# Two held sums that change places, a join moved by one slot, and a sum moved by one slot with a weight behind it

## The chip, the cores and the metric

The kernel runs on one core of a Trainium2 chip. The metric is the device time of one execution in microseconds; a stated time is the median of three runs unless it is said to be that of the profiled execution. Five engines of the core matter here: TensorE (PE in the profile; its weight loads are PEld), VectorE (DVE), ScalarE (ACT), GpSimd (POOL) and SyncE (SP), which issues nearly all DMAs.

## The reference

One layer of a hybrid block over a sequence of 1024 tokens with 1024 channels, in float32:

```
h = rms_norm(x, norm1_g);  z = h @ w_in              # 1024 x 7168 columns
glu_in, q, k, v, gate_logits = split(z)
a = a_val * sigmoid(a_gate)                          # GLU
a = silu(rms_norm(causal_depthwise_conv(a, width 31) + conv_b));  y_a = a @ w_conv_out
q, k = rms_norm per head (16 heads of 64)
for window, dilation in ((128, 1), (512, 4), (2048, 16)):   # three dilated windows, ALiBi slopes
    scores -> softmax -> o_g, lse_g
o = sum_g softmax(lse)_g * o_g;  y_b = o @ w_attn_out
x = x + (sigmoid(g_a) * y_a + sigmoid(g_b) * y_b) @ w_out
x = x + conv-GLU feed-forward (w_up, width-3 convolution, w_down)
```

## The kernel before

Every float32 product is made of three fp32r matmuls: an operand is split into a high part (a rounding copy, on ACT) and a low part (the rest, by a subtraction on DVE), and high x high, high x low and low x high are accumulated. `split` makes such a pair, `wpiece` loads a weight into one of four `raw` buffers, which are used in turn, and splits it.

The stages in order are: the first norm and the first GLU columns; the remaining GLU and half of the gate columns in pairs (71 to 285 us in the profile); Q, K and V, with the depthwise convolution on DVE, ACT and POOL beside both stages (to 567 us); the attention heads, with the other gate columns and the convolution's output product as filler (to 857 us); the merge of both branches; the output product; and the feed-forward part. In most of them the order of the instructions on ACT, DVE and PE (in the heads on POOL too) is the order written by hand (`tc.manual_schedule`); the other engines, SP's DMA queue among them, and the stretches between are ordered by a planner that simulates the kernel. `tc.issue_after(ins)` puts what is issued in its block behind `ins` on that engine.

**The pairs.** `PAIRS` has eleven pairs of column blocks, computed with a scheme of seven products instead of eight per pair: five GLU pairs, then six gate pairs. For each pair, PE accumulates into the PSUM bank X (half of `xz[n]`) and the bank Y (`spare_bank`), and two partial results are held in the two halves of the SBUF tile `pq`: `c12` (first half) and `p5` (second half). ACT copies X into `c12` (line 828), PE then forms Y, ACT copies Y into `p5` (line 834), PE goes on accumulating into X, DVE adds X to `p5` (line 719, a helper of `tt_`). For a gate pair `p5` is then spilled to DRAM (line 841); near the end of the pair DVE adds Y to `c12` and that is spilled (line 876). For a GLU pair, `last_v1` runs in the next pair: a sigmoid over `c12` in place (line 873), then one DVE product that reads both halves (line 874).

**The heads.** Work goes in slots, eight per head: slots 0 to 3 of a head score the first half of the queries, slots 4 to 7 the second half (slot 4 is the group "far", the second half's queries against the first half's keys at the larger dilation, lines 1091 to 1093). A slot on PE scores its blocks into one of two PSUM banks that alternate by slot (lines 1055, 1056); DVE takes the score plus mask and its minimum in one instruction (`least`, line 1059); ACT takes the exponentials (`powers`, line 1100). `BACK` = 12 slots later the same block is transposed on PE (`flip`, line 1152), split by ACT and DVE (lines 1173, 1174) and, one or two slots after that, multiplied with V (`weigh`, lines 1190, 1191). For the second half of the queries the far part and the rest have a softmax each, and the two are joined in between: DMAs bring each part's statistics to the other (lines 1117, 1120, 1124), `compare` (lines 1128, 1129, on DVE) runs at slot 4 + 8 of a head's own count, `combine` (one exponential on ACT, three DVE instructions to line 1137, then eight scalings on POOL, line 1103) one slot later. Slots in which a head is scored, and slots 12 later in which it is transposed, overlap with the next heads.

**The end of the heads.** Thirteen slots run after the last score. In some of them `o_step` advances the attention output's first half, in four parts: the sum of the two partial results that the heads left in DRAM (`raw_o`, line 1227, DVE), high part (line 1223, ACT) and low part (line 1220, DVE), each one step of `o_step` apart; a part's load is `o_fetch`. After that come the first four weights of the attention output (`ao_first`, `raw_ao`), planned behind the last low part (`settled_o[3]`), then the four parts of the second half through the same `raw` buffers, and the merge: sigmoids of two gates on ACT (lines 1342, 1343), PE's product `yb` into one of four banks (lines 131 to 133), and DVE's use of that bank (line 1351).

Of the kernel before, what the change touches and what calls it, by code (L numbers as in the profile page):

```python
# [15 lines left out]
AF = mybir.ActivationFunctionType  # L16
ALU = mybir.AluOpType
# [20 lines left out]
BACK = 12  # L38
# [31 lines left out]
def block_kernel(ctx: ExitStack, tc: tile.TileContext, x, xT, x0, g2, pack, mask,  # L70
                 w_first, w_ch, w_qkv, w_co, w_ao, w_o, w_up, w_down, out):
    nc = tc.nc
    act, dve, pool, pe, sp = nc.scalar, nc.vector, nc.gpsimd, nc.tensor, nc.sync
# [21 lines left out]
    shared = []  # L95
# [17 lines left out]
    def wpiece(src, name, raw=None):  # L113
        raw = stage(src, name) if raw is None else raw
        hi, lo = wsplit(raw, name)
        if len(src.shape) == 3:
            hi = hi.rearrange("p (a b) -> p a b", a=src.shape[1])
            lo = lo.rearrange("p (a b) -> p a b", a=src.shape[1])
        return hi, lo
# [199 lines left out]
    if True:  # L319
# [131 lines left out]
        turns = lambda t: t.rearrange("p (m s) -> p s m", s=2)  # L451
# [33 lines left out]
        a, b = range(4), range(4, 8)  # L485
# [91 lines left out]
        gating, ready = [True], []  # L577
# [191 lines left out]
        half_of = lambda c, half: apad[c][:, :, 15 + half * 256 : 15 + half * 256 + 256]  # L769
# [4 lines left out]
        with tc.issue_after(settled1.ins), tc.manual_schedule(engines=hand):  # L774
            padded(2)
            gv = [big_ps(f"glu{n}_2") for n in "gv"]
            for half in (1, 0):
                for ps, w in zip(gv, w2):
                    for _ in gemm_half(ps[:, half * 512 : half * 512 + 512], w, hT, half):
                        pass  # L780
            for n, which in ((0, 0), (0, 1)):
                load(n, which)
            token_sums(0)
            parts(0, 0, "v")
            token_sums(1)
            load(1, 0)
            sg = [cst.tile([P, 512], F32, tag="f2", bufs=2, name=f"sg_2_{half}") for half in range(2)]
            act.activation(sg[1], gv[0][:, 512:1024], AF.Sigmoid)
            sums(0)
            token_form("t2", 0)  # L790
            dve.tensor_tensor(out=half_of(2, 1), in0=turns(gv[1][:, 512:1024]), in1=turns(sg[1]), op=ALU.mult)
            token_form("t2", 1)
            act.activation(sg[0], gv[0][:, 0:512], AF.Sigmoid)
            dve.tensor_tensor(out=half_of(2, 0), in0=turns(gv[1][:, 0:512]), in1=turns(sg[0]), op=ALU.mult)
            parts(1, 0, "v")
            parts(0, 2, "s12")
            pair_first(0)
            for i in range(2):
                token_form("t1", i)
            pq = p1.tile([P, CW - 1 + T], F32, tag="apad", bufs=9, name="pq")  # L800
            c12, p5 = pq[:, 0:512], pq[:, 512:1024]
            parts(0, 1, "s3")
            begun(0)
            for i in range(2):
                token_form("t3", i)
            pair_first(1)
            for n, (a, b) in enumerate(PAIRS):
                X = xz[n][:, 0:512]
                Y = spare_bank
                (sh, sl), (gh, gl) = pw[n]["s12"], pw[n]["s3"]  # L810
                inner = 0 < n < N - 1
                glu = n < len(GLU)
                if n + 2 < N:
                    load(n + 2, 0)
                if n + 1 < N:
                    load(n + 1, 1)
                parts(n, "s4", "s4")
                if n == 0:
                    begun(1)
                    for i in range(2):  # L820
                        tt_(xts[1][2 + i], xts[0][2 + i], xts[1][2 + i], sub)
                if inner:
                    parts(n + 1, 0, "v")
                if 0 < n <= len(GLU):
                    last_v1()
                odd_add()
                product(X, sh[:, 4:8], sl[:, 4:8], *form["t2"], False)
                act.activation(c12, X, AF.Copy)
                if n == 0:
                    for i in range(2):  # L830
                        token_form("t4", i)
                conv(PULLS[0] if n else 0)
                product(Y, sh[:, 0:4], sl[:, 0:4], *form["t1"], True)
                act.activation(p5, Y, AF.Copy)
                conv(PULLS[1] if n else 0)
                if inner:
                    odd(ODD_PAIR[1], False)
                product(X, gh[:, 0:4], gl[:, 0:4], *b12, False)
                tt_(p5, X, p5, add)
                if not glu:  # L840
                    sp.dma_start(dgate[b - 16][:, 512:1024], p5)
                if n + 1 < N:
                    sums(n + 1)
                if inner:
                    pair_first(n + 1)
                    parts(n + 1, 2, "s12")
                    odd_add()
                    conv(PULLS[2])
                    begun(n + 1)
                    conv(PULLS[3])  # L850
                else:
                    product(Y, *pw[n]["s4"], *b22, False)
                    tt_(c12, Y, c12, add)
                    if n + 1 < N:
                        parts(n + 1, 2, "s12")
                paired = product(X, gh[:, 4:8], gl[:, 4:8], *form["t4"], False)
                if glu:
                    padded(b)
                    dve.tensor_tensor(out=half_of(b, 0), in0=turns(X), in1=turns(c11[n]), op=ALU.mult)
                else:  # L860
                    c21 = cst.tile([P, 512], F32, tag="f2", bufs=2, name=f"c21_{n}")
                    act.activation(c21, X, AF.Copy)
                    sp.dma_start(dgate[b - 16][:, 0:512], c21)
                if inner:
                    product(Y, *pw[n]["s4"], *b22, False)
                if n + 1 < N:
                    parts(n + 1, 1, "s3")
                odd(ODD_PAIR[0], False)
                if inner:
                    tt_(c12, Y, c12, add)  # L870
                if glu:
                    def last_v1(c=b):
                        act.activation(c12, c12, AF.Sigmoid)
                        shared[:] = [dve.tensor_tensor(out=half_of(c, 1), in0=turns(p5), in1=turns(c12), op=ALU.mult)]
                else:
                    sp.dma_start(dgate[a - 16][:, 512:1024], c12)
        for i in range(2):
# [21 lines left out]
        def qkv_tail(ch, tt, qn):  # L899
# [13 lines left out]
            for s, t in ((0, qh), (1, ql)):  # L913
# [13 lines left out]
        slots = [[wp.tile([P, 1024], F32R, tag=f"w{a}", bufs=4, name=f"qkv_{a}{i}") for a in ("hi", "lo")]  # L927
                 for i in range(4)]
# [98 lines left out]
    if True:  # L1027
# [81 lines left out]
        own, other, shares = {}, {}, {}  # L1109
# [99 lines left out]
        def o_fetch(half, k):  # L1209
            cs = slice(half * 512, half * 512 + 512)  # L1210
            part = lambda i: do_[k : k + 2, i, :, cs].rearrange("k p t -> p k t")
            raw = stage(part(0), f"o_{half}{k}").rearrange("p (a b) -> p a b", a=2)
            hi, lo = (oT[i][half][:, k : k + 2, :] for i in range(2))
            fetch(lo, part(1))
            return raw, hi, lo

        def o_step(new):
            if o_highs:
                raw, hi, lo = o_highs.pop()
                settled_o.append(dve.tensor_tensor(out=lo, in0=raw, in1=hi.bitcast(F32), op=ALU.subtract))  # L1220
            if o_sums:
                raw, hi, lo = o_sums.pop()
                act.activation(hi, raw, AF.Copy)
                o_highs.append((raw, hi, lo))
            if new:
                raw, hi, lo = new.pop(0)
                dve.tensor_tensor(out=raw, in0=raw, in1=lo.bitcast(F32), op=ALU.add)
                o_sums.append((raw, hi, lo))
# [10 lines left out]
        with tc.manual_schedule(engines={ENG.Activation, ENG.DVE, ENG.PE, ENG.Pool}):  # L1239
# [3 lines left out]
            for at in range(len(slots) + BACK + 1):  # L1243
# [34 lines left out]
                    result(*done)  # L1278
                    done = None
                for ago, ready in ((BACK - 3, combine), (BACK - 4, compare)):  # L1280
                    if 0 <= at - ago < len(slots) and slots[at - ago][1:] == (1, 0):
                        ready(slots[at - ago][0])
                for unit in new:
                    powers(*unit)
                if cur is not None and half == 0:
# [7 lines left out]
                    oT = [[hb2[0].tile([P, KT, 512], F32R, tag=f"hb{a}0", name=f"oT{a}0")] for a in range(2)]  # L1293
                    heads = [o_fetch(0, k) for k in range(0, KT - 2, 2)]
                if at - len(slots) in (4, 5, 8, 9, 10, 11, 12):
                    o_step(heads)
                if at == len(slots) + BACK - 4:
                    heads.append(o_fetch(0, KT - 2))
                if apart(at):
                    piece_low()  # L1300
                with tc.issue_after(last_v.ins) if not at else ExitStack():
# [19 lines left out]
    if True:  # L1321
        for a in range(2):
            oT[a].append(hb2_tile([P, KT, 512], F32R, f"hb{a}1", f"oT{a}1"))
        with tc.issue_after(settled_o[3].ins):
            ao_first = [wpiece(w_ao[c], f"ao{c}") for c in range(4)]
        for k in range(0, KT, 2):
            later = [o_fetch(1, k)]
            for _ in range(3):
# [606 lines left out]
```

## Time and profile before

| | |
|---|---|
| median of three runs | 1672.17 us (1672.17 to 1672.96) |
| profiled execution | 1673.21 us, span 1671.0 us |
| instructions | 23004 |
| granted TensorE clock | 1.000 |
| PE busy | 1658.8 us, 99% of the span |
| DVE busy | 1244.5 us, 74% |
| ACT busy | 918.8 us, 55% |
| POOL busy | 406.4 us, 24% |
| chain that ended last | PE 91%, DMA 3%, DVE 3%, ACT 1%, issue 1% |
| DMA over the span | 290.84 MB, 174 GB/s |

A busy share is an average over the stages. PE's share says that it is at work nearly all the time; where it is not, the list of who waited for whom names the places, and the timeline around each place shows what was in front. In a timeline row the columns are start, duration, engine, line, operation, result <- operands, shape and count; the bracket at the end is the engine's idle time before it and what ended it. A matmul's duration is modelled and longer than the step from one matmul to the next, so PE's idle times in brackets are shorter than the true gaps by the difference.

### The profile page before, as it was taken

Reading aid. Unit: us, or ns where it says so; the run is one execution under the profiler, and the core shown is the slowest. Engines: PE = TensorE matmul, PEld = TensorE weight load, DVE = VectorE, ACT = ScalarE, POOL = GpSimd, SP = SyncE. Lnnn points to the kernel's source line nnn. Section 1 sums busy time; section 2 is a strip of 40 time slices with the busy share of each in tenths; the row PEclk is TensorE's granted clock in tenths of the full one; section 3 lists DMA queues with packets and bytes.
Section 4 is the critical chain, followed back from the end, with each engine's and each line's share of the span. In section 5 each row is a group of like instructions: output and inputs, shape, how many; then the busy total and the mean of one; then the engine's idle time right before and its main releaser. Section 6 shows DMA issues by size and latency. Waiting matters only on the chain.

```text
span 1671.0 us, 23004 instructions
## 1 busy us (share of the span) xinstructions
PE 1658.8 (99%) x7867; PEld 1383.8 (83%) x7867; DVE 1244.5 (74%) x1996; ACT 918.8 (55%) x1748; POOL 406.4 (24%) x450
## 2 busy tenths in 40 slices
PE   9999999999999999999999999999999999999999
PEld 7888778888888888888888888888888888888887
DVE  6999887879784567867567645878776777789863
ACT  6555445776665578777646434555444544543431
POOL 0024344877752256455410000000000000000000
PEclk9999999999999999999999999999999999999999
DMA  9111335344345879888678594522222222598851
GB/s 358 39 51 51 100 108 198 95 131 163 114 133 182 303 237 299 264 262 246 173 266 288 202 327 167 176 86 89 89 76 88 76 86 90 162 390 293 281 171 51
DMA packets 182341, 290.84 MB, mean 174 GB/s; under 512 B 31952, under 2 KB 89936, under 8 KB 181712
## 3 DMA queue, kind: packets, MB, share of 16 engines
q1 hardware_dynamic: 180928, 285.05, 51.5%
q10 hardware_dynamic: 1296, 4.33, 0.6%
q8 instruction: 62, 1.02, 0.3%
q14 instruction: 55, 0.45, 0.1%
HBM read 209.50 MB, written 79.76 MB: 173 GB/s over the span
## 4 chain that ended last, share of the span: by engine, by line
PE 91%; DMA 3%; DVE 3%; ACT 1%; issue 1%; POOL 0%; SPq 0%; ACTq 0%; DVEq 0%; POOLq 0%
PE dx L1741 7%; PE xz L158 6%; PE xz L156 6%; PE xz L157 6%; PE dy L1741 5%; PE qkv L150 5%; PE qkv L148 5%; PE qkv L149 5%; PE y L158 2%; PE y L157 2%; PE y L156 2%; PE gx L156 2%; PE gx L158 2%; PE gx L157 2%; PE pp L1152 2%; PE wo L149 2%
## 5 line engine op out<-in xcount | busy, mean ns | idle before, releaser
L572 POOL TENSOR_TENSOR codd<-codd,cpart 128x513 f32<-128x513 f32 x112 | 147.8, 1321 | 136.3 <-DVE lo_s L100 58.6
L148 PE MATMUL qkv<-qkv_hi,hT 128*128 128x512 f32 x384 | 152.7, 398 | 0.0
L150 PE MATMUL qkv<-qkv_hi,hT 128*128 128x512 f32 x384 | 150.3, 391 | 0.0
L149 PE MATMUL qkv<-qkv_lo,hT 128*128 128x512 f32 x384 | 149.9, 390 | 0.0
L1644 DVE SCALAR_TENSOR_TENSOR u<-u,pk 128x1023 f32<-128x1023 f32 x88 | 112.1, 1276 | 1.2 <-ACT u L1642 0.9
L621 DVE SCALAR_TENSOR_TENSOR conv<-csum,both,conv 128x512 f32<-128x512 f32 x120 | 90.1, 751 | 2.3 <-ACT conv L653 0.3
L621 DVE SCALAR_TENSOR_TENSOR conv<-apad,pk,conv 128x512 f32<-128x512 f32 x120 | 90.0, 750 | 1.6
L150 PEld LDWEIGHTS qkv<-qkv_hi,hT 128*128 128x128 f32 x384 | 72.0, 188 | 15.7
L149 PEld LDWEIGHTS qkv<-qkv_lo,hT 128*128 128x128 f32 x384 | 72.3, 188 | 14.5
L148 PEld LDWEIGHTS qkv<-qkv_hi,hT 128*128 128x128 f32 x384 | 72.2, 188 | 14.2
L100 DVE TENSOR_TENSOR lo_uv<-raw_uv,hi_uv 128x1024 fp32r<-128x1024 f32 x20 | 24.5, 1225 | 79.6 <-ACT hi_uv L99 79.6
L1174 DVE TENSOR_TENSOR pl<-pp,ph 128x512 fp32r<-128x512 f32 (+1 forms) x95 | 58.8, 619 | 30.3 <-ACT ph L1173 29.3
L586 ACT ACTIVATE cpart<-apad,pk 128x513 f32<-128x513 f32 x112 | 76.6, 745 | 2.0 <-POOL codd L572 1.5
L1059 DVE CUSTOM_DVE_ANT_0 p<-s,m 128x512 f32<-128x512 f32 (+1 forms) x120 | 59.0, 502 | 21.8 <-POOL p L1103 16.6
L156 PE MATMUL xz<-h2left,hi_uv 128*128 128x512 f32 x176 | 68.6, 390 | 0.0
L156 PE MATMUL xz<-blk_t,hi_s3g 128*128 128x512 f32 x176 | 68.5, 389 | 0.0
L158 PE MATMUL xz<-blk_t,lo_s3g 128*128 128x512 f32 x176 | 68.5, 389 | 0.0
L157 PE MATMUL xz<-blk_t,hi_s3g 128*128 128x512 f32 x176 | 68.5, 389 | 0.0
L158 PE MATMUL xz<-h2left,lo_uv 128*128 128x512 f32 x176 | 68.5, 389 | 0.0
L157 PE MATMUL xz<-h2left,hi_uv 128*128 128x512 f32 x176 | 68.5, 389 | 0.0
L1173 ACT ACTIVATE ph<-pp 128x512 fp32r<-128x512 f32 (+1 forms) x95 | 51.1, 538 | 26.1 <-PE pp L1152 25.5
L124 POOL TENSOR_TENSOR rs<-ss,mhalf 128x8 f32<-128x8 f32 x32 | 53.6, 1676 | 36.5 <-DVE ss L123 34.4
(479 smaller groups left out, 5184.4 us busy)
## 6 DMA issues: line engine op xcount, KB each, us to landing
wr<-w_down SPq DMA_DIRECT2D x45, 512.0 KB, 5.6
kk<-dk SPq DMA_DIRECT2D x32, 512.0 KB, 6.1
gr<-dff SPq DMA_DIRECT2D x62, 256.0 KB, 5.4
raw_qkv<-w_qkv SPq DMA_DIRECT2D x24, 512.0 KB, 4.7
raw_g<-w_ch SPq DMA_DIRECT2D x23, 512.0 KB, 3.7
dff<-u SPq DMA_DIRECT2D x22, 512.0 KB, 2.6
raw_uv<-w_up SPq DMA_DIRECT2D x21, 512.0 KB, 3.6
raw_ug<-w_up SPq DMA_DIRECT2D x20, 512.0 KB, 3.6
```

Of the source, the lines that this page charges most:

```text
L148: pe.matmul(ps, ah, hi[:, k % 2, :], start=(k == 0), stop=False)
L149: pe.matmul(ps, ah, lo[:, k % 2, :], start=False, stop=False)
L150: end = pe.matmul(ps, al, hi[:, k % 2, :], start=False, stop=(k == KT - 1))
L156: pe.matmul(o, wh[:, k, :], bh[:, k, :], start=(start and k == 0), stop=False, skip_group_check=not start)
L157: pe.matmul(o, wh[:, k, :], bl[:, k, :], start=False, stop=False, skip_group_check=not start)
L158: end = pe.matmul(o, wl[:, k, :], bh[:, k, :], start=False, stop=(k == 3), skip_group_check=not start)
L572: r = pool.tensor_tensor(out=out, in0=in0, in1=in1, op=op)
L586: act.activation(part, zo[:, i : i + 513], AF.Copy, scale=taps[:, c, 2 * i + 1 : 2 * i + 2])
L621: dve.scalar_tensor_tensor(out=out_, in0=src[:, i : i + 512], scalar=w, in1=out_, op0=ALU.mult, op1=ALU.add)
L1059: dve.tensor_tensor_reduce(out=pt, in0=s, in1=m, scale=-1.0, scalar=3e38, op0=ALU.add, op1=ALU.min, accum_out=nm)
L1644: dve.scalar_tensor_tensor(out=acc[:, d:], in0=src[:, : T - d], scalar=w(2 - d), in1=acc[:, d:], op0=ALU.mult, op1=ALU.add)
L1741: pe.matmul(banks[n][:, cols], a[:, c], b[:, d], start=(start and i == 0 and m == 0), stop=(stop and i == nf - 1 and m == 2), skip_group_c ...
```

## The change

Three edits, in three places.

The first: the two halves of `pq` are put in a list `held`, and a pair with an odd number takes them in reverse order as `c12` and `p5`. `last_v1`, which runs in the next pair, is given the two halves of its own pair.

The second: in the slots before `BACK + 4` = 16, `compare` and `combine` look one slot further back, so for the first head they run one slot later, in slots 13 and 14 instead of 12 and 13. Later heads are as before.

The third: in the ninth slot after the last score `o_step` starts no new sum; the fourth sum, and its high and low part, come one slot later each. In the eleventh such slot the first attention-output weight `ao0` is loaded and split in the hand-written order, so its high part follows the fourth high part on ACT, and its low part stands ahead of the fourth low part on DVE. The other three weights stay behind that low part.

```diff
-            c12, p5 = pq[:, 0:512], pq[:, 512:1024]
+            held = [pq[:, 0:512], pq[:, 512:1024]]
...
                 (sh, sl), (gh, gl) = pw[n]["s12"], pw[n]["s3"]
+                c12, p5 = held[::-1] if n % 2 else held
...
-                    def last_v1(c=b):
-                        act.activation(c12, c12, AF.Sigmoid)
-                        shared[:] = [dve.tensor_tensor(out=half_of(c, 1), in0=turns(p5), in1=turns(c12), op=ALU.mult)]
+                    def last_v1(c=b, own=(c12, p5)):
+                        act.activation(own[0], own[0], AF.Sigmoid)
+                        shared[:] = [dve.tensor_tensor(out=half_of(c, 1), in0=turns(own[1]), in1=turns(own[0]), op=ALU.mult)]
...
                 for ago, ready in ((BACK - 3, combine), (BACK - 4, compare)):
-                    if 0 <= at - ago < len(slots) and slots[at - ago][1:] == (1, 0):
-                        ready(slots[at - ago][0])
+                    then = at - ago - (at < BACK + 4)
+                    if 0 <= then < len(slots) and slots[then][1:] == (1, 0):
+                        ready(slots[then][0])
...
                 if at - len(slots) in (4, 5, 8, 9, 10, 11, 12):
-                    o_step(heads)
+                    o_step(heads if at - len(slots) != 9 else [])
                 if at == len(slots) + BACK - 4:
                     heads.append(o_fetch(0, KT - 2))
+                if at == len(slots) + BACK - 1:
+                    ao_first = [wpiece(w_ao[0], "ao0")]
...
         with tc.issue_after(settled_o[3].ins):
-            ao_first = [wpiece(w_ao[c], f"ao{c}") for c in range(4)]
+            ao_first += [wpiece(w_ao[c], f"ao{c}") for c in range(1, 4)]
```

## The prediction

> **What bounds the kernel now.** I read the page first, then who waited for whom on PE, then the chain of waits in order of time, then the timeline at each place where PE stands still.
>
> ```profile
> PE 1658.8 (99%) x7867; PEld 1383.8 (83%) x7867; DVE 1244.5 (74%) x1996; ACT 918.8 (55%) x1748; POOL 406.4 (24%) x450
> ...
> PE gx L156 <- ACT pq L828: 3.3, 4, 1.6
> PE s L1055 <- DVE own L1059: 2.1, 1, 2.1
> PE o L1191 <- DVE pl L1174: 1.3, 1, 1.3
> ...
> PE yb L131 <- DVE gg L1351: 0.2, 1, 0.2
> ```
>
> PE is the bound at 99%, and the diff removes no matmul. So all it can win is PE's pauses, and these four rows, 6.9 us of 1671, are most of them. The first three are the three edited places. What counts at each is not whether the named wait goes, but which wait ends last once it is gone.
>
> **Part A: the two held sums change places from pair to pair.**
>
> ```profile
> 192.74 5.25 DMA dgate<-pq
> ...
> 196.57 0.39 PE L157 MATMUL spare<-gt,hi_s 128*128 128x512 f32 x1
> 196.79 0.39 PE L158 MATMUL spare<-gt,lo_s 128*128 128x512 f32 x1
> 198.10 0.60 ACT L828 ACTIVATE pq<-gx 128x512 f32<-128x512 f32 x1 [4.80 <-DMA dgate<-pq]
> 198.59 0.59 ACT L834 ACTIVATE pq<-spare 128x512 f32<-128x512 f32 x1
> 198.75 0.50 PE L156 MATMUL gx<-hT,hi_s 128*128 128x512 f32 x1 [1.57 <-ACT pq L828]
> 199.09 0.39 PE L157 MATMUL gx<-hT,hi_s 128*128 128x512 f32 x1
> 201.89 0.69 DVE L719 TENSOR_TENSOR pq<-gx,pq 128x512 f32<-128x512 f32 x1 [3.50 <-PE gx L158]
> L841 SPq DMA_DIRECT2D dgate<-pq x6: 319/320/376, 181.7 to 281.6; - x6
> DMA to landing us min/median/max: 2.0/2.6/9.9
> ```
>
> In a pair of gate columns the copy of X into `c12` (L828) cannot start until the spill of the previous pair's `c12` has been read out: ACT stands 4.80 us, PE needs X back and stands too. PE's steady step is 0.23 us (196.57 to 196.79; the starts are rounded), so the pause at 198.75 is 198.75 - 196.79 - 0.23 = 1.73 us. The list counts from a matmul's modelled end, 0.39 after its start, so its 3.3 us over four pauses is 3.3 + 4 x 0.16 = 3.95 us, and each restart costs 0.11 more (198.75 to 199.09 is 0.34). Together 4.4 us.
>
> After the edit, `c12` of a pair goes where the pair before held `p5`, whose spill (L841) left at 181.7 for the pair shown, 11 us before `c12`'s own spill and so more than 11 us before the new copy; the longest landing of any spill of this tile is 9.9 us. So this wait goes. What is late next: the copy into `p5` (L834) now meets the late spill. It could start when product Y ends, 196.79 + 0.39 = 197.2, and waits to 198.1. Behind it on ACT stand convolution copies, which started after 198.59 + 0.59 before and so lose nothing. Its reader is the sum at L719, which waited 3.50 us for PE and can now start at 201.89 - 1.84 = 200.05; `p5` is there by 198.1 + 0.6 = 198.7. Covered by 1.3 us. For the five GLU pairs the last product of the pair before reads both halves in one DVE instruction, so the exchange changes nothing there: 0. If the two halves were tracked as one tile, A would be worth 0; against a loss stands that no instruction is added. I take 4.4, ends 0 and 4.4.
>
> Arriving 4.4 us early could uncover the depthwise convolution, which POOL and DVE run beside. Its consumer is at 512.5:
>
> ```profile
> 506.64 1.29 POOL L572 TENSOR_TENSOR sqacc<-sqacc,csq 128x512 f32<-128x512 f32 x1
> 512.51 1.84 PE L685 MATMUL conv<-ones,sqacc 128*128 128x1 f32 x16
> ```
>
> POOL's sum ends at 507.9, 4.6 us ahead of PE, and DVE and ACT, which feed it, follow PE's order. A's gain stays.
>
> **Part B: the first head's softmax join, one slot later.**
>
> ```profile
> 580.00:600.00 20.00, 17.84 (x101) 14.70 (x100) 12.90 (x53) 13.99 (x43) 9.67 (x16) 1.00 0.65 189
> ...
> 587.27 0.39 PE L1055 MATMUL s<-kk,q 128*128 128x512 f32 x1
> 591.86 0.17 DVE L1128 TENSOR_TENSOR both<-own,other 128x8 f32<-128x8 f32 x1 [3.88 <-DMA dstat<-own]
> 592.14 0.68 DVE L1059 CUSTOM_DVE_ANT_0 p<-s,m 128x512 f32<-128x512 f32 x1
> 592.75 0.55 DVE L1174 TENSOR_TENSOR pl<-pp,ph 128x384 fp32r<-128x384 f32 x1
> 592.89 0.39 PE L1055 MATMUL s<-kk,q 128*128 128x256 f32 x1 [2.14 <-DVE own L1059]
> 593.73 0.51 DVE L1059 CUSTOM_DVE_ANT_0 p<-s,m 128x384 f32<-128x384 f32 x1
> 593.91 1.41 POOL L1103 TENSOR_SCALAR pf_first<-pf_first,both 128x128 f32<-128x128 f32 x4 [6.05 <-DVE both L1137]
> 595.29 2.16 POOL L1103 TENSOR_SCALAR p_first<-p_first,both 128x512 f32<-128x512 f32 x4
> 595.68 0.60 PE L1152 MATMUL pp_far<-ident,pf_first 128*128 128x128 f32 x4
> 597.62 0.60 PE L1152 MATMUL pp<-ident,p_first 128*128 128x128 f32 x4
> ```
>
> `compare` (L1128) holds DVE 3.88 us until the other half's statistics land; behind it stands the minimum L1059 over a score that PE wrote at 587.27, and PE waits for that bank: 2.14 + 0.16 = 2.3 us, 2.4 with the restart. One slot later, that minimum (0.68) and a low half (0.55) run before `compare`, in its waiting time, and this wait goes. But the landing does not move, and the join feeds what PE transposes next. Chain after: `compare` at 591.86 as now, then the next slot's minimum (0.51) and low half (0.55) instead of 0.68 + 0.55, then `combine`: it ends 0.17 earlier. POOL's scalings then end near 597.3 instead of 595.29 + 2.16 = 597.45, and the transposes at 597.62 need the last of them for their second block, 0.1 later. With PE 2.3 us early it stops at 595.68 - 2.3 = 593.4 for `pf_first` (last piece at 593.91 + 1.41 - 0.17 = 595.15) and again for `p_first`: the pause moves, and that second block's 597.7 becomes about 597.4. I take 0.3; ends 0 (nothing but the landing counts) and 2.4 (POOL's part would not count). SP: its spills of the next head's statistics and the loads behind them wait for exponentials that come up to 4 us earlier now; that may help later heads a little, and I leave it out of the sum.
>
> **Part C: the last sum of the heads' parts a slot later, a weight behind it.**
>
> ```profile
> 852.00:856.00 4.00, 2.86 (x15) 2.40 (x16) 3.99 (x6) 3.35 (x5) 0.00 (x0) 1.00 0.65 201
> 866.00:868.00 2.00, 2.00 (x11) 1.65 (x10) 0.98 (x1) 0.00 (x0) 0.00 (x0) 1.00 1.05 407
> ...
> 851.39 1.22 DVE L1227 TENSOR_TENSOR raw_o<-raw_o,oT 128x1024 f32<-128x1024 f32 x1 [1.05 <-DMA oT<-do]
> 851.41 0.42 PE L1190 MATMUL o<-ph,v 128*128 128x384 f32 x1
> 853.14 0.44 PE L1191 MATMUL o<-pl,v 128*128 128x384 f32 x1 [1.31 <-DVE pl L1174]
> 854.23 0.69 DVE L1174 TENSOR_TENSOR pl<-pp,ph 128x512 fp32r<-128x512 f32 x1
> 854.98 0.38 PE L1191 MATMUL o<-pl,v 128*128 128x256 f32 x1
> 855.97 2.35 DVE L100 TENSOR_TENSOR lo_ao<-raw_ao,hi_ao 128x1024 fp32r<-128x1024 f32 x2
> ...
> 856.11 5.52 DMA raw_ao<-w_ao
> 864.42 8.90 DMA oT<-do
> ...
> 876.51 2.28 SPq L104 DMA_DIRECT2D raw_ao<-w_ao  x4
> 879.16 0.50 PE L131 MATMUL yb<-oT,hi_ao 128*128 128x512 f32 x1 [0.19 <-DVE gg L1351]
> ```
>
> The sum L1227 waits for a landing and holds DVE; the low half `pl` behind it is late; PE loses 853.14 - 851.41 - 0.23 = 1.5 us. In the new order DVE, free at 851.39 - 1.05 = 850.34, does `pl` (0.55, above), a low part (1.2, half of the 2.35), the sum (1.22, its data landed) and the next `pl` (0.69): 3.66 us, less 0.07 where one starts before the other's end (592.14 + 0.68 against 592.75), done near 853.8. PE wants that one at 851.6 + (854.98 - 853.14) = 853.4, so 0.4 comes back at once; 1.1 is left.
>
> But the chain of waits runs from here through DMA to PE's pause at 879.16 (0.19 + 0.16 + 0.11 restart = 0.46): a weight's load leaves at 856.11 when the last low part has freed its buffer, and its split frees the buffer of the last second-half part, loaded at 864.42. The new order puts the weight's high and low part ahead of that last low part. After the sum (now ended near 853.1) come a high part, the weight's high part, its low part and then the last low part, at most 1.2 us each: it ends near 857.7, and that load leaves 1.6 us later. Two ends: the whole 1.6 arrives at 879.16 (C = -1.6), or nothing does and both pauses go (C = 1.1 + 0.46 + the 0.4 = 1.9). I take a value by the nearest row: at 866 the DMA share is 1.05 at 407 GB/s and the part needs 8.90 us, so it stands in a full queue, about 3.6 MB deep, and leaving 1.6 us later does not change when the queue gets to it. On the other side the third weight leaves about 2 us earlier, into the stretch at 852 to 856 where the share is only 0.65. So PE resumes near 879.0 whenever it arrives: C = 0.2.
>
> [...]
>
> **Sum.** 4.4 + 0.3 + 0.2 = 4.9 us. The profiled execution took 1673.21 us (span 1671.0), 1.04 above the median of 1672.17; taken from the median it gives 1667.3.
>
> **Rivals.**
> 1. The pauses go whole: POOL's scalings or the queue do not hold PE. 4.4 + 2.4 + 0.2 to 1.9 is 7.0 to 8.7: 1663.5 to 1665.2. For it: the list names DVE, not POOL. Against: 597.45 against 597.71.
> 2. The later weight arrives in full, or the queue runs dry before the parts: C = -1.6 to -3 (the dry time, 0.35 x 4 us, added). Sum 1.7 to 3.1: 1669.1 to 1670.5.
> 3. A does nothing because the halves count as one tile: 0.5 us, 1671.7. Against: the copy of `p5` ran at 198.59 right behind the other.
> 4. Slower. Only ACT, DVE, PE and POOL are ordered by hand, and only up to there; what follows is placed by a planner that sees a changed end. If it puts the splits of the second four weights (issued from 876.51; at 5.52 us for the first and 1.29 for each 512 KB behind it at 407 GB/s the last lands near 885.9) ahead of the first gates' sigmoids on ACT, PE resumes near 889, with 3 of the 5.84 us behind it that now lie between the last part's landing (864.42 + 8.90) and 879.16. That is 10 us lost: 1672.17 - 4.7 + 10 = 1677. It decides for slower from 8 us on. Against: before, they are issued last.
>
> The Trainium skill, TensorE: Matmul & The Clock Gate, Part 1, halves PE's clock after some 3.4 us without work; by that a pause as in rival 4 costs about 1.7 us more. No pause here is that long: the stretch with the longest shows 1.00.
>
> **How the numbers follow.** Forecast 0.52 (own range 1666.0 to 1668.8), rival 1 0.16, rival 2 0.17, rival 3 0.05, rival 4 0.06, small reorderings 0.04. 0.2% is 3.3 us, about what a measurement of this kernel can tell from no change. Faster: forecast, rival 1 and part of the rest, 0.73; same: rivals 2 and 3, 0.20; slower 0.07. The range 1663.8 to 1670.0 takes the forecast, nearly all of rival 1 and most of 2.
>
> **What would show it.** A: no row of PE waiting for L828, and L834 waiting for the DMA. B: PE waiting at L1152 for POOL, near 1.7 us; DVE's minimum ahead of L1128. C: no 1.3 us row at L1191, a longer one at `yb`. Wrong if PE waits longer at `yb` than it saved, or if L1152 shows no wait.

## The result, and the profile after

The changed kernel took 1668.26 us in the median of ten runs (1665.41 to 1669.63), the kernel before 1672.17 us (1670.07 to 1673.68); the ratio, taken over all the runs and so not quite that of the two medians, is 0.9975, with a 95% interval of 0.9966 to 0.9985, a gain of 4.2 us (2.5 to 5.7). The prediction was 1667.3 us, a gain of 4.9. The profiled execution of the changed kernel took 1668.18 us (span 1666.0). Lines behind the edits are one to four higher than before: L828 is L829, L1059 is L1060, L1152 is L1153, L1191 is L1192, L1351 is L1355.

PE's busy time is the same within 1 us, 1658.0 us. The list of PE's waits has changed in all three edited places:

```profile
PE yb L131 <- DVE gg L1355: 1.2, 1, 1.2
PE glu L446 <- ACT whi_gv L436: 1.1, 1, 1.1
...
PE pp_far L1153 <- POOL pf_first L1104: 0.7, 1, 0.7
PE o L1192 <- DVE pl L1175: 0.2, 1, 0.2
```

`gx` no longer waits for the copy out of X, the score no longer waits for DVE, and `o` waits 0.2 us instead of 1.3. In their place stand a wait for POOL at `pp_far` and a longer one at `yb`.

Edit 1, in the timeline of the changed kernel at the pair that the prediction showed:

```profile
195.52 0.60 ACT L829 ACTIVATE pq<-gx 128x512 f32<-128x512 f32 x1 [1.20 <-PE gx L158]
...
197.81 0.39 PE L158 MATMUL spare<-gt,lo_s 128*128 128x512 f32 x1
198.04 0.39 PE L156 MATMUL gx<-hT,hi_s 128*128 128x512 f32 x1
198.66 0.60 ACT L835 ACTIVATE pq<-spare 128x512 f32<-128x512 f32 x1 [2.54 <-DVE conv L621]
```

The copy follows the product (it waits for PE, not for the spill) and ends at 196.12, 1.9 us before PE needs X: 197.81 to 198.04 is PE's ordinary step. The second copy (L835) starts 0.46 us after the product's end (198.20); the list names DVE, but the late spill also landed only then, at 198.56. PE does not wait for it.

Edit 2, in the timeline of the changed kernel around the first head's join:

```profile
584.60 0.69 DVE L1060 CUSTOM_DVE_ANT_0 p<-s,m 128x512 f32<-128x512 f32 x1
588.71 0.17 DVE L1129 TENSOR_TENSOR both<-own,other 128x8 f32<-128x8 f32 x1 [2.69 <-DMA dstat<-own]
590.62 1.41 POOL L1104 TENSOR_SCALAR pf_first<-pf_first,both 128x128 f32<-128x128 f32 x4 [6.11 <-DVE both L1138]
591.05 1.37 PE L1153 MATMUL pp_far<-ident,pf_first 128*128 128x128 f32 x4 [0.72 <-POOL pf_first L1104]
592.01 2.16 POOL L1104 TENSOR_SCALAR p_first<-p_first,both 128x512 f32<-128x512 f32 x4
593.77 1.00 PE L1153 MATMUL pp<-ident,p_first 128*128 128x128 f32 x4
```

The minimum runs in the waiting time (584.60), DVE still waits for the landing, and PE follows POOL piece by piece: `pp_far` takes 1.37 us instead of 0.60, the second `pp` 1.00 instead of 0.60. A comparison of the two traces matmul by matmul (start after minus start before) shows it as a sum: -3.4 us ahead of the join, -5.8 with the score's pause gone, -3.9 behind `pp_far`, -3.5 behind `pp`. Of the 2.4 us, 2.3 come back within 5 us.

Edit 3, in the chain of waits of the changed kernel from the last head to PE's pause at `yb`:

```profile
850.35 1.24 DVE lo_ao L100
851.60 4.69 DMA raw_ao<-w_ao
...
857.40 1.24 DVE lo_ao L100
859.07 9.14 DMA oT<-do
868.30 1.24 DVE raw_o L1228
869.57 0.59 ACT oT L1224
870.65 1.28 ACT L1346
871.94 0.72 ACT gg L1346
872.67 0.62 ACT gg L1347
873.31 0.70 DVE gg L1355
874.06 0.50 PE yb L131
```

A weight's low part (857.40) is the last thing ahead of the load, as foreseen. That weight's own load left at 851.60, when the first weight's low part (850.35) had freed a buffer, and not behind the last low part of the sums, as the prediction had it. Between the landing at 868.21 and PE lie 5.85 us of DVE, ACT (L1346 at 870.65 is a table load for the sigmoid) and DVE again. By matmuls the difference of the traces goes from -4.8 before the heads' end to -6.0 behind it and to -5.1 behind `yb`: the heads' end gains 1.2 and `yb` takes 0.9 back.

### The profile page after: what moved, and what is told of

Its sections match the earlier page's. It is cut to its first block, busy times and chain, and to the rows that moved or that the text cites. A ratio compares the mean times of both kernels' runs of the same rounds, so it can differ in the third digit from the quotient of the medians.

```text
span 1666.0 us, 23008 instructions
## 1 busy us (share of the span) xinstructions
PE 1658.0 (100%) x7867; PEld 1384.3 (83%) x7867; DVE 1244.6 (75%) x1996; ACT 919.6 (55%) x1748; POOL 406.5 (24%) x450
## 4 chain that ended last, share of the span: by engine, by line
PE 96%; DMA 1%; DVE 1%; issue 1%; ACT 1%; POOL 0%; SPq 0%; POOLq 0%; DVEq 0%; ACTq 0%
PE dx L1745 7%; PE xz L156 6%; PE xz L158 6%; PE xz L157 6%; PE dy L1745 5%; PE qkv L150 5%; PE qkv L148 5%; PE qkv L149 5%; PE gx L158 3%; PE gx L156 3%; PE gx L157 3%; PE y L156 2%; PE y L158 2%; PE y L157 2%; PE pp L1153 2%; PE wo L150 2%
## 5 line engine op out<-in xcount | busy, mean ns | idle before, releaser
L1060 DVE CUSTOM_DVE_ANT_0 p<-s,m 128x512 f32<-128x512 f32 (+1 forms) x120 | 59.1, 503 | 21.7 <-POOL p L1104 16.2
```

Source lines behind the costliest of these rows:

```text
L1060: dve.tensor_tensor_reduce(out=pt, in0=s, in1=m, scale=-1.0, scalar=3e38, op0=ALU.add, op1=ALU.min, accum_out=nm)
```

## The experiments

**The three edits one by one, and the kernel before once more.** All are compared with the same runs of the kernel before (1672.83 us).

Edit 1 alone:

```diff
-            c12, p5 = pq[:, 0:512], pq[:, 512:1024]
+            held = [pq[:, 0:512], pq[:, 512:1024]]
...
+                c12, p5 = held[::-1] if n % 2 else held
...
```

> The kernel before with the first edit alone: the two held sums change places from pair to pair. Theory 1 (each edit acts at its own place, and the later pauses of the heads were shortened by the second edit): the four pauses behind the copy of X are gone, 4.5 us in the trace between the first and the last pair; the 2.3 us pause at 593 stays, the pauses near 661 to 675 stay at about 1.3 us in all, those at 851 and 879 stay. Median near 1672.2 - 4.5 = 1667.7. Theory 2 (the 1.3 us near 661 to 675 belong to the first edit, or come and go from execution to execution): they are gone or changed here too.

Measured: 1668.4 us (1666.83 to 1672.72), ratio 0.998 (0.9971 to 0.9988), a gain of 3.3 us (2.0 to 4.8). PE waits for L829 nowhere; at the score it still waits 2.7 us, at `o` 1.2. At one of the gate pairs the second copy waits for the late spill, as the prediction had foretold, and PE does not wait for that copy:

```profile
198.45 0.60 ACT L835 ACTIVATE pq<-spare 128x512 f32<-128x512 f32 x1 [2.91 <-DMA dgate<-pq]
```

Edit 2 alone:

```diff
-                    if 0 <= at - ago < len(slots) and slots[at - ago][1:] == (1, 0):
-                        ready(slots[at - ago][0])
+                    then = at - ago - (at < BACK + 4)
+                    if 0 <= then < len(slots) and slots[then][1:] == (1, 0):
+                        ready(slots[then][0])
```

> The kernel before with the second edit alone: the first head's join one slot later. Theory 1: the pause for the score's bank goes and comes back at the far part's transposes and at the next ones, net 0.0 to 0.3 us there; then 1.3 us more near 661 to 675, because SP's queue, which stood behind exponentials held up by the join, sends the next heads' loads earlier. Median near 1670.8. Theory 2: nothing near 661 to 675, median near 1672.1.

Measured: 1670.57 us (1668.52 to 1672.47), 0.9989 (0.9981 to 0.9998), a gain of 1.8 us (0.3 to 3.2). At its own place the trace gives 0.3 us: against the kernel before, its matmuls start 0.3 us earlier ahead of the join, 2.6 behind the score and 0.6 behind `pp`. The runs give more than the place.

Edit 3 alone:

```diff
-                    o_step(heads)
+                    o_step(heads if at - len(slots) != 9 else [])
...
+                if at == len(slots) + BACK - 1:
+                    ao_first = [wpiece(w_ao[0], "ao0")]
...
-            ao_first = [wpiece(w_ao[c], f"ao{c}") for c in range(4)]
+            ao_first += [wpiece(w_ao[c], f"ao{c}") for c in range(1, 4)]
```

> The kernel before with the third edit alone: last sum a slot later, the first weight behind it. Theory 1: the pause of 1.5 us at the heads' end becomes 0.25, and the pause before the fifth product of the merge becomes 1.3 instead of 0.35, because what it waits for comes out of a full DMA queue at the same time as before; net 0.2 to 0.4 us, median near 1671.9. Theory 2 (the pause at the merge in the changed kernel was lengthened by another edit): net 1.2 us or more, median 1671.0 or below.

Measured: 1671.44 us (1669.93 to 1674.86), 0.9997 (0.9988 to 1.0006). Its trace has both sides in PE's waits:

```profile
PE yb L131 <- DVE gg L1353: 2.1, 1, 2.1
...
PE o L1191 <- DVE pl L1174: 0.2, 1, 0.2
```

What `o` gains (1.3 to 0.2) `yb` takes, and more (0.2 to 2.1). By the starts of the matmuls this execution loses 0.6 us between the heads' end and `yb`, where 0.2 to 0.4 had been expected as a gain.

The kernel before, unchanged:

> The kernel before, unchanged, for a second trace of it beside the single edits: how much its pauses and its first loads differ from one execution to the next. Theory 1: the pauses at 198 to 278, 593, 661 to 675, 851 and 879 are the same within 0.2 us, and only the time of the first matmuls (PE's waits for the first weights, 0 to 2 us) differs. Theory 2: the pauses near 661 to 675 differ by a microsecond.

Measured: 1672.41 us (1671.35 to 1673.13), 1.0001 (0.9992 to 1.0009). It shows two things that one profiled execution of the kernel before had not. First, some of what separates the two first traces belongs to no edit. Some 1.3 us of short pauses between 661 and 675 us, absent after the change, are mostly absent here too and with each edit alone; so a theory that an edit brings that gain falls. And the pause of the pairs, 3.3 us in the list before, is smaller in each of the other traces that have it:

```profile
PE gx L156 <- ACT pq L828: 2.7, 4, 1.4
PE s L1055 <- DVE own L1059: 2.3, 1, 2.3
```

It is 2.5 us with edit 2 alone and 2.1 with edit 3 alone. Second, in the timeline of this execution PE is slow after the pause at the score:

```profile
592.62 0.39 PE L1055 MATMUL s<-kk,q 128*128 128x256 f32 x1 [2.28 <-DVE own L1059]
...
593.43 0.42 PE L132 MATMUL gate<-hT,hi_gt 128*128 128x512 f32 x1
593.66 0.61 PE L133 MATMUL gate<-hT,lo_gt 128*128 128x512 f32 x1
...
595.99 0.63 PE L1055 MATMUL s<-kk,q 128*128 128x512 f32 x1
...
596.84 0.73 PE L1152 MATMUL pp_far<-ident,pf_first 128*128 128x128 f32 x4
```

Matmuls of 512 columns follow at 0.43 us instead of 0.23, from 593.7 to 596.8. The windows of the same trace give the granted clock (the third number from the end):

```profile
592.00:594.00 2.00, 1.39 (x7) 1.27 (x8) 1.93 (x9) 1.40 (x4) 0.36 (x2) 0.92 0.00 0
594.00:597.00 3.00, 3.00 (x9) 2.36 (x8) 1.13 (x5) 2.17 (x7) 3.00 (x8) 0.50 0.48 133
597.00:600.00 3.00, 3.00 (x21) 2.72 (x20) 2.03 (x6) 2.17 (x5) 2.54 (x4) 0.99 0.87 283
```

Half clock from 594 to 597. Over the whole span this is a mean granted clock of 0.999 (1.67 us in 1671), and every timed run lists that mean. Of the 74 runs of the kernel before in all three sets of runs, 42 are at 1.000 (median 1671.36 us) and 32 below (1673.56). So the hypothesis was: the pause at the score costs not only its 2.4 us but, in about half of the executions, 2 us more, and edit 2, which only breaks the pause into pieces, takes these away. The next experiments ask for it from both sides.

**The statistics read earlier, without edit 2 and with it.** SP issues the read of the far half's statistics (`other<-dstat`) one slot earlier for the first head, ahead of the next head's loads:

```diff
-                for ago, n0, send in ((2, 0, far_out), (1, 3, near_to_far), (READ, 0, far_to_near)):
+                for ago, n0, send in ((2, 0, far_out), (1, 3, near_to_far), (READ - (at < BACK), 0, far_to_near)):
```

> The changed kernel, with SP's read of the far half's statistics (other<-dstat) issued one slot earlier for the first head, ahead of the next head's loads instead of behind them. The theory (the end of part B's wait is the landing, as the prediction's lower end says): the landing, which ends DVE's wait at L1129 at 588.71, comes about 3 us earlier, so the join's scalings on POOL end earlier by more than the pauses at pp_far (0.7 + 0.35 us) and at pp: both go, about 2 us less than the changed kernel, 1666.3 by the fast runs of it. The rival (POOL's scalings or DVE's order hold PE whenever the landing comes): the row of pp_far <- pf_first stays at 0.4 us or more and the time is that of the changed kernel, 1668.3.

Measured: 1666.73 us (1665.68 to 1669.74), 0.9967 (0.9956 to 0.9978). The timeline of the compare in this kernel:

```profile
587.44 0.17 DVE L1129 TENSOR_TENSOR both<-own,other 128x8 f32<-128x8 f32 x1 [2.06 <-DMA other<-own]
```

The landing came earlier by 1.3 us, not 3, and it is another DMA that ends it now: the near half's statistics (`other<-own`), which I had not counted, stand behind the same loads. PE waits 0.9 us at the score instead of 0.7 at `pp_far`, and gains 0.6 us on the changed kernel across the join. The time lies 1.5 us under the changed kernel's, with overlapping intervals; the place accounts for 0.6 of it.

The same without edit 2:

> Edits 1 and 3 with the early read, and without edit 2: the join stays in its old slot and the statistics come earlier. Two things are asked. If DVE stood at the compare for the landing alone, the pause of 2.1 to 2.7 us at the score's matmul (s <- own) is gone or below 0.5 us, 2.4 us of edit 2's upper end without edit 2. And the clock: without edit 2 the kernels ran about half of their executions below a granted clock of 1.000 (before 16 of 35, edit 1 alone 5 of 12, edit 3 alone 6 of 11), with it 1 of 21. Theory: it is the unbroken pause of 2.3 us or more that drops the clock; without that pause nearly all executions show 1.000, and the time is 1666 to 1667. Rival: the clock comes from somewhere else (edit 2's different order, or the chip's temperature); then about half stay below 1.000 and the median is 1 us higher.

Measured: 1668.73 us (1666.73 to 1671.99), 0.9977 (0.9967 to 0.9987). The pause did not go, for the same reason:

```profile
588.10 0.17 DVE L1129 TENSOR_TENSOR both<-own,other 128x8 f32<-128x8 f32 x1 [4.13 <-DMA other<-own]
...
589.13 0.39 PE L1056 MATMUL s<-kk,q 128*128 128x256 f32 x1 [2.36 <-DVE own L1060]
```

So it could not test the clock by removing the pause. It tests it in the other direction: pause 2.36 us, no edit 2, and 7 of 10 runs below 1.000 (their median 1669.85 us, that of the other three 1667.89).

**The join's combine right behind its compare**, on top of the change:

```diff
-                for ago, ready in ((BACK - 3, combine), (BACK - 4, compare)):
-                    then = at - ago - (at < BACK + 4)
+                joins = ((BACK - 3, combine), (BACK - 4, compare))
+                for ago, ready in joins[::-1] if at < BACK + 4 else joins:
+                    then = at - ago - (at < BACK + 4 and ready is compare)
```

> The changed kernel, with the first head's combine right behind its compare in the same slot, instead of a minimum and a low half between them: POOL's scalings start some 1.1 us earlier, while the next score's minimum (0.5 to 0.7 us) and low half come that much later. Theory (the join's scalings on POOL are what part B's remainder waits for): the pause at pp_far gets 0.7 + 0.35 us shorter, down to nothing, and the one at pp by up to 0.5; 1667.2. Rival (the pause only changes its place): PE waits at a score again for DVE, 1 us or more in a row s <- own, and the time is that of the changed kernel, 1668.3, or above it by what the low half holds up.

Measured: 1667.41 us (1665.96 to 1669.12), 0.997 (0.9958 to 0.9981), all six runs at clock 1.000. PE's rows at the join:

```profile
589.04 0.50 PE L1056 MATMUL s<-kk,q 128*128 128x512 f32 x1 [0.31 <-DVE own L1060]
...
589.73 0.72 PE L1153 MATMUL pp_far<-ident,pf_first 128*128 128x128 f32 x4
...
591.82 1.00 PE L1153 MATMUL pp<-ident,p_first 128*128 128x128 f32 x4
```

`pp_far` is back to 0.72 us and waits for nobody; 0.31 has moved to the score, and the second `pp` still takes 1.00. Across the join PE gains 1.0 us on the changed kernel. At this place the theory holds, the rival in a small part: what PE stood for was the end of POOL's scalings. The time itself cannot be told from the changed kernel's (0.997 against 0.9975), and the trace has a new wait of 1.3 us at the first `yb` product, for the weight's high part on ACT, which the expectation did not have.

**The last sum moved, the weight left behind it:**

```diff
-                if at == len(slots) + BACK - 1:
-                    ao_first = [wpiece(w_ao[0], "ao0")]
...
-            ao_first += [wpiece(w_ao[c], f"ao{c}") for c in range(1, 4)]
+            ao_first = [wpiece(w_ao[c], f"ao{c}") for c in range(4)]
```

> The changed kernel, with the last sum of the heads' parts a slot later but the first output weight's high and low part left out of the hand's order, behind it where the planner puts them, as before the change. Theory of part C in the prediction (a full DMA queue sets when PE resumes at yb, the 1.6 us of the weight's later split do not arrive): the same time within 0.4 us, and PE resumes at yb within 0.5 us of the changed kernel, counted from the heads' end. Rival (the landing follows its issue, 2 us plus the bytes): the last second-half part leaves some 1.6 us earlier, PE's wait at yb falls from 1.2 to 0 and the time falls by 1.2 to 1.6 us, to 1667.

Measured: 1667.71 us (1666.1 to 1669.84), 0.9972 (0.9961 to 0.9983): as the changed kernel. The profiled execution, at 1669.84 the longest of its six, fits neither theory:

```profile
850.00 0.51 PE L131 MATMUL yb<-oT,hi_ao 128*128 128x512 f32 x1 [0.75 <-ACT hi_ao L99]
...
850.58 0.28 PE L1192 MATMUL o<-pl,v 128*128 128x256 f32 x1
...
854.98 0.50 PE L131 MATMUL yb<-oT,hi_ao 128*128 128x512 f32 x1 [1.84 <-ACT hi_ao L99]
```

The planner put the first `yb` product ahead of the last head's `o`, and PE then waited for the weight's high part, here and at 854.98. The order on PE changed, which I had not foreseen, so this run does not tell the two theories apart.

**A pause put back.** If the clock follows the pause, a pause made by other means must bring the drop back, with edit 2 in place. First at the same place: the compare repeats its last small instruction ten times.

```diff
-            dve.tensor_scalar(f, f, 80.0, None, op0=ALU.min)
+            for _ in range(1 if h else 11):
+                dve.tensor_scalar(f, f, 80.0, None, op0=ALU.min)
```

> The changed kernel, in which the first head's compare repeats its last instruction (the minimum with 80 on 128x8, 0.2 us each) ten times more, about 2.0 us on DVE. It puts an unbroken pause of PE back at the place of the first head's join: the next score's minimum ends 2 us later, so PE stands at the score's matmul (s <- own) for 2.0 to 2.5 us, and again up to 1 us at pp_far. By the row alone this costs 2.0 us: 1670.3. Theory of the clock (an unbroken pause of PE above 2 us makes the clock drop in about half of the executions; so far 48 of 96 without edit 2 and 4 of 39 with it): 4 or more of 10 executions below 1.000, and those 1.5 to 2 us longer; 1671 in the median. Rival (edit 2 works on the clock in another way than by the length of the pause): at most 1 of 10 below 1.000, 1670.3.

Measured: 1669.26 us (1667.27 to 1672.8), 0.9984 (0.9975 to 0.9993), and 7 of 11 runs below 1.000. The landing was early in the profiled execution, and PE's pause shorter than aimed at, in two pieces:

```profile
PE s L1056 <- DVE own L1060: 1.4, 1, 1.4
...
PE pp_far L1154 <- POOL pf_first L1104: 0.7, 1, 0.7
```

Still the clock fell, in the windows of the same trace:

```profile
590.00:593.00 3.00, 2.22 (x10) 1.41 (x9) 1.62 (x8) 2.19 (x8) 2.48 (x6) 0.83 1.00 357
593.00:595.00 2.00, 2.00 (x7) 1.66 (x7) 1.33 (x4) 1.47 (x4) 2.00 (x4) 0.50 0.86 235
```

So "unbroken above 2 us" was too narrow: in this execution two pauses of 1.4 and 0.7 us, two matmuls apart, were enough, with `pp_far` at POOL's pace (1.53 us) behind them. How long the pauses of the other ten were is not known. The time is below what was expected (1671), since the pause was.

Then at quite another place: one pair of gate columns copies X nine times.

```diff
-                act.activation(c12, X, AF.Copy)
+                for _ in range(9 if n == 6 else 1):
+                    act.activation(c12, X, AF.Copy)
```

> The changed kernel, in which one pair of gate columns (the seventh) copies X nine times into its held sum instead of once. In the changed kernel PE has X back 1.9 us after the copy's end (196.12 to 198.04); eight more copies at 0.5 to 0.6 us are 4.0 to 4.7 us, so PE stands about 2.1 to 2.8 us unbroken at its next product, some 395 us ahead of the heads. Cost by the row: 2.1 to 2.8 us, 1670.4 to 1671.1. Theory of the clock (any unbroken pause of 2 us and more): 4 or more of 10 executions below 1.000 and 1 us more in the median. Rival (the drop belongs to the heads' place or its load): at most 1 of 10 below 1.000.

Measured: 1672.51 us (1669.97 to 1675.37), 1.0002 (0.9993 to 1.0011), and 10 of 11 runs below 1.000, three of them below 0.999. PE's timeline:

```profile
200.15 0.50 PE L156 MATMUL gx<-hT,hi_s 128*128 128x512 f32 x1 [3.01 <-ACT pq L830]
...
201.26 0.63 PE L157 MATMUL gx<-hT,hi_s 128*128 128x512 f32 x1
...
204.61 0.39 PE L156 MATMUL gx<-hT,hi_v 128*128 128x512 f32 x1
```

Eight matmuls from 201.26 to 204.61 take 3.35 us instead of 8 x 0.23 = 1.84: 1.5 us lost behind the pause. The pause was longer than expected (3.0 us instead of 2.1 to 2.8), and so was the time. The drop belongs to the pause, not to the heads.

The counts together, in runs whose clock is listed: with the score's pause (the kernel before, edit 1 or 3 alone, the early read without edit 2) 57 of 118 below 1.000; with edit 2 and no pause put back 4 of 45; with a pause put back 7 of 11 and 10 of 11. With edit 2 alone, where four pauses of the pairs up to 1.0 us remain in the list, 0 of 11. One count points the other way: the kernel with the weight left behind has a pause of 1.8 us at `yb` in its profiled execution, and 1 of 6 runs below 1.000. The Trainium skill, TensorE: Matmul & The Clock Gate, Part 1, has a free-running window of about 3.4 us, and the clock halved after one idle window. That the drop comes in some executions only and lasts 3.35 us agrees with a window that runs on its own; that 2.3 us, or 1.4 and 0.7 with work between, are enough does not agree with a window that must be wholly idle.

The listed clocks also allow a comparison with the drop left out. Among the executions at 1.000 alone, the medians are 1671.29 us for the kernel before (19 runs), 1667.59 with edit 1 (7), 1670.57 with edit 2 (all 11) and 1670.01 with edit 3 (5): gains of 3.7, 0.7 and 1.3 us. The unchanged kernel once more gives 1671.87 (4 runs), 0.6 us from its own first number, so differences below a microsecond are not settled by this. For edit 2 the gain is 0.7 instead of 1.8 us: some 1.1 us go with the clock.

**The first merge's gates loaded ahead**, with the combine behind the compare, as the version that the experiments point to:

```diff
...
+        gg0 = p3.tile([P, 3, 512], F32, tag="e", bufs=3, name="gg_0_0")
+        sp.dma_start(gg0[:, 0], dgate[0][:, 0:512])
+        sp.dma_start(gg0[:, 1], dgate[8][:, 0:512])
+        sp.dma_start(gg0[:, 2], dya[0][:, 0:512])
         for k in range(0, KT, 2):
             later = [o_fetch(1, k)]
...
```

> The changed kernel with the first head's combine right behind its compare (1667.4 in its own run) and with the gates and the first half's part of the first merge loaded ahead of the last second-half parts, into a buffer of their own. Theory (PE's pause at yb, 1.2 us, 1.5 with its restart, waits for what lands last in the full queue, and the first gates are among it): PE no longer waits at yb and the time is 1666.0. Rival (the queue is full, so what is loaded earlier pushes the last second-half part back by as much as it brings): the pause at yb stays or grows by up to 1.8 us (three loads of 256 KB at 407 GB/s) and the time is 1667.4 to 1669.

Measured: 1665.88 us (1665.39 to 1669.34), 0.9966 (0.9954 to 0.9978), all six runs at 1.000. The list of PE's waits has no `yb`:

```profile
PE s L1056 <- DVE own L1060: 1.1, 1, 1.1
...
PE o L1192 <- DVE pl L1175: 0.2, 1, 0.2
```

and the timeline on ACT and DVE says why:

```profile
861.16 0.72 ACT L1352 ACTIVATE gg<-gg,pk 128x512 f32<-128x512 f32 x1
...
871.36 1.22 DVE L1228 TENSOR_TENSOR raw_o<-raw_o,oT 128x1024 f32<-128x1024 f32 x1
872.61 1.06 ACT L1224 ACTIVATE oT<-raw_o 128x1024 fp32r<-128x1024 f32 x1 [2.43 <-DVE raw_o L1228]
```

The last part's sum now runs at 871.36, 3.1 us later than in the changed kernel, and PE does not stand. So the product at `yb` does not need the last part; it needs the first merge's sigmoids, which came behind that part's high part on ACT and now run at 861.16. In the changed kernel the two gates had landed at 870.11 and 871.42, behind the last part (868.21). This run moved their loads, and the order on ACT moved with them; which of the two freed PE it does not tell. The gain over the changed kernel's own run, 2.4 us, has overlapping intervals; at the places its trace shows 1.4 us at `yb` and only 0.2 at the join, where the landing came later in this execution (PE waits 1.1 us at the score).

## Why the prediction was right, point by point

**The total.** 4.9 us forecast, 4.2 (2.5 to 5.7) measured. That the two agree so well is in part luck: the first term was too large by some 0.7 us, the second lacked some 1 us that the clock costs, and the third cannot be told from nothing.

**Edit 1 was sized too large.** The mechanism is as foretold: no row of `gx` waiting for L829. The 4.4 us are what the two first traces show at the pairs (4.6). But they were read from one profiled execution, and it had the longest pauses of the four that were profiled with them (3.3 us in the list against 2.7, 2.5 and 2.1). Added up as in the prediction, with 0.27 for each of the four pauses, the four executions give 4.4, 3.8, 3.6 and 3.2, in the mean 3.7; edit 1 alone gained 3.3 (2.0 to 4.8), and 3.7 in the executions at clock 1.000. The interval alone would not exclude 4.4. The sign foretold for the second copy, L835 waiting for the DMA, showed in the trace of edit 1 alone, at one pair (2.91 us), and cost PE nothing, as foretold; in the changed kernel the list names PE and DVE's `conv` there.

**Edit 2 was right at its place and short of an effect elsewhere.** 0.3 us was forecast and 0.1 to 0.3 is what the traces show there; PE's wait at `pp_far` for POOL, forecast at 1.7 us, is 0.7 in the list and 1.9 with the pieces that PE then takes at POOL's pace. The step that failed is the last sentence on the clock, behind the rival "slower": "No pause here is that long: the stretch with the longest shows 1.00." The profiled execution had kept its clock after that pause; 32 of 74 others had not. At 2.2 us in 43% of the executions this is 1.0 us on average, and 0.3 + 1.0 fits the 1.8 (0.3 to 3.2) of edit 2 alone. That such a pause brings the clock down is shown by the two kernels with a pause put back, and without the clock's drop the gain is 0.7 instead of 1.8; to better than about a microsecond the intervals do not divide it.

**Edit 3 cannot be told from nothing, and two of its steps were wrong.** 0.2 was forecast; edit 3 alone gained 0.5 (-1.0 to 2.0). The pause at `o` goes and the one at `yb` grows, as foretold, but the sum changes from one execution to the next: between the heads' end and `yb` the changed kernel gains 0.3 us on the first trace and edit 3 alone loses 0.6, while the three traces without this edit differ from that first trace by 0.1 to 0.6 us at the same place (the kernel before again gains 0.6, edit 1 alone 0.4, edit 2 alone loses 0.1). The first wrong step is that the weight's load leaves 1.6 us later. It left at 851.60 instead of 856.11, 4.5 us earlier where PE was 4.8 us earlier, so it was only 0.3 us late, for it no longer waited for the last low part. The second is that PE's return at `yb` needs the last second-half part: in the last kernel that part is 3 us later and PE does not wait. It counted in the changed kernel because the sigmoids stood behind it on ACT. Whether leaving later means landing later in that queue stays open: the last part's load left 5.3 us earlier than in the trace before and landed 5.1 us earlier (8.90 against 9.14 us from issue to landing), so there was hardly a delay to be hidden, and the experiment with the weight left behind changed PE's order instead.

**The rivals.** The pauses going whole (1) is refuted by `pp_far` and `yb`; the price of the later weight arriving in full (2) was paid in part with edit 3 alone (2.1 us at `yb`), but there the last part's load took 10.34 us to land instead of 8.90. The pairs' edit doing nothing (3) and the planner's misplacement (4) did not occur. Short changes in the first weights' arrival (PE waits 1.1 us at `glu` in one execution and not in another) and the 1.3 us at 661 to 675 move single executions by as much as edits 2 and 3; a difference of two traces is no measure of these without its place.

## What to carry to other kernels

A pause of the bound engine is not priced by its length alone: list the granted clock of every run, not of the profiled one, and look at the spacing of the matmuls right behind the longest pause. Moving an instruction out of a waiting engine's way gains only as far as the data that end the wait are not needed next: find the next reader before counting the pause as won, and if all readers need the landing, move the landing, with every DMA that the waiting instruction reads. Before a pause is taken as a term, see it in a second execution.

## What the runs showed of the hardware that was not expected

- Kernels with the score's pause (1.9 to 2.7 us in the lists of their profiled executions) showed a mean granted clock below 1.000 in 57 of 118 runs, the one with a pause of 3.0 us in 10 of 11. Where a trace caught it, the clock was one half for about 3.4 us (all of 594 to 597 and parts of the windows beside it). Each drop costs some 1.5 us by the matmuls' spacing; in the kernel before the medians of runs with and without it lie 2.2 us apart.
- One execution with two pauses of 1.4 and 0.7 us, two matmuls apart, had it, and 7 of 11 runs of that kernel; the changed kernel (0.7 us with POOL's pace behind it) and edit 2 alone (that and pauses of 1.0 us far apart) had it in 1 of 21.
- Reads of a few bytes (the statistics) land behind the loads issued ahead of them on the same queue: issued at 582.68 behind them in the changed kernel, `other<-dstat` landed at 588.49, 5.8 us later; issued at 579.69 ahead of the next head's loads, it took 2.0 us and no longer ended the wait, and another such read, still behind them, did.
